# The opening of a two-layer decoder trunk: each gate unit for both token tiles in turn, and one product in native float32

## The chip, the core and the metric

The program runs on one core of one Trainium2 chip. The metric is the device time of one execution in microseconds (us); the time before is 909.27 us, the median of three runs (908.61 to 909.62). Times inside an execution are counted from the start of its profiled span.

## What is computed

Two layers, each of three sub-layers on 256 tokens of 1024 numbers: a SwiGLU feed-forward block, a mixer with parallel heads, and a second feed-forward block. Every sub-layer has a norm ahead of it and behind it.

```python
def _swiglu(h, wg, wu, wd):
    return (jax.nn.silu(h @ wg) * (h @ wu)) @ wd

for l in range(DEPTH):                       # DEPTH 2, D_MODEL 1024, D_FF 2816, SEQ 256
    f = _swiglu(_rmsnorm(h, ff1_norm_pre[l]), ff1_w_gate[l], ff1_w_up[l], ff1_w_down[l])
    h = h + 0.5 * _rmsnorm(f, ff1_norm_post[l])
    m = _hybrid_mixer(_rmsnorm(h, mix_norm_pre[l]), ...)
    h = h + _rmsnorm(m, mix_norm_post[l])
    f = _swiglu(_rmsnorm(h, ff2_norm_pre[l]), ff2_w_gate[l], ff2_w_up[l], ff2_w_down[l])
    h = h + 0.5 * _rmsnorm(f, ff2_norm_post[l])
```

All is float32. The change touches only the first columns of `h @ wg` and `h @ wu` in the first feed-forward block of the first layer, the first thing that the kernel does.

## The kernel before

**Split products.** A float32 operand is held as two tiles in a shorter format, an upper part `hi` (a copy into float32r by ScalarE, ACT, L117) and a lower part `lo` (the difference, by VectorE, DVE, L118). A product is then three: x-upper by `hi`, x-lower by `hi`, x-upper by `lo`. The x side is split too, into the two halves of `xT` (L258 on ACT, L259 on DVE). Every weight goes through ACT and DVE once on its way to the matrix engine (PE).

**Units and buffers.** Weights come in units of 1 MB (128 x 2048) by DMAs issued on the SyncE queue (SP, L85) into five `raw` buffers; a load waits until its buffer's last unit has been read. `Weights.split_next` splits the next unit into one of five `hi`/`lo` pairs; the units of the opening are split in four pieces of 512 columns, later ones in two of 1024.

**The opening.** The 256 tokens are two tiles t=0 and t=1 of 128. Per tile the normed x is turned by PE (L309, four 128x128 transposes into one PSUM bank, for each of two halves of the 1024 features). The first four units are the first 512 gate columns (units 0 and 1, for the two halves of the features) and the first 512 up columns (units 2 and 3). `ffn_first(t)` makes for one tile the gate product with units 0 and 1, then the up product with units 2 and 3 (`mm_half`, L398, 24 matmuls of 128x512 for each product), takes the SiLU of the first on ACT (L500) and multiplies on DVE (L490, the gate; its result is `hf`). All of tile 0 is made first, then all of tile 1. PE turns tile 1's x during tile 0's up product. Ahead of the first product PE runs six and later five matmuls on zeros (L233), which only keep it busy.

**Behind the opening.** The next four products (`ffn_quad`, L607) are a Strassen-like scheme: its weight units are sums (DVE, L113 and L136, in place in a `raw` buffer, then split like the others), its x operands are sums of quarters of x, split into tiles `n` (L258, L259); these come from copies `left` of tile 0's turned x and from tile 1's PSUM banks. Between the first and the second of these products PE turns the second tile's `hf` (`turn_tile`, L548), so its queue waits there for the second gate. The first tile's `hf` is turned by a DMA (`send`, L524) instead.

**What sets the order.** Each engine runs its own queue in the order in which the build's scheduler put the instructions; `tc.issue_after` and `tc.keep_in_program_order` constrain it. What stands in a queue can be read from the built program.

Of the kernel before, what the change touches and what calls it, by code (L numbers as in the profile page):

```python
# [10 lines left out]
F32 = mybir.dt.float32  # L11
# [3 lines left out]
AF = mybir.ActivationFunctionType  # L15
ALU = mybir.AluOpType
AX = mybir.AxisListType

P = 128
# [150 lines left out]
def hybrid_trunk_kernel(ctx: ExitStack, tc: tile.TileContext, a, out: bass.AP):  # L170
# [128 lines left out]
            nc.vector.scalar_tensor_tensor(xn[i], h[:, t, s], r, gain[i] if gain else gains[:, 0, s], op0=ALU.mult, op1=ALU.mult)  # L299
        return xn  # L300

    def pre_turn(t, xn, left=None, between=None):


        turned = []
        for i in range(2):
            ps = bank()
            for k in range(4):
                pre_turn.last = nc.tensor.transpose(ps[:, k * P : (k + 1) * P], xn[i][:, k * P : (k + 1) * P], ident)  # L309
            at = (slice(None), slice(4 * i, 4 * i + 4), slice(t * P, (t + 1) * P))  # L310
            split_into(xT, at, ps.rearrange("p (k n) -> p k n", k=4))
            pre_turn.lower = split_into.lower
            turned.append(ps)
            if between and not i:
                between()

        def keep():
            for i in range(2):
                left[i] = buf()
                nc.scalar.activation(left[i], turned[i], AF.Copy)  # L320

        if left is None:
            return
        if t == 0:
            return keep if between else keep()

        def part(name, x):
            left[name] = (buf(F32R, tag="n"), buf(F32R, tag="n"))
            split_into(left[name], (slice(None), slice(None)), x)
            left[name] = [y.rearrange("p (k n) -> p k n", k=4) for y in left[name]]  # L330

        s1, s3 = buf(), buf()
        x11, x12 = left.pop(0), left.pop(1)

        def rest():
            part("S3", s3)
            nc.vector.tensor_tensor(x12, x12, x11, op=ALU.add)
            part("S4", x12)

        def middle():  # L340
            part("S1", s1)
            nc.vector.tensor_tensor(x11, s1, x11, op=ALU.subtract)
            part("S2", x11)

        nc.scalar.activation(s1, turned[1], AF.Copy)
        nc.vector.tensor_tensor(s1, turned[0], s1, op=ALU.subtract)
        nc.vector.tensor_tensor(s3, x11, turned[0], op=ALU.subtract)
        left["middle"], left["rest"] = middle, rest
        for i, (name, k, t_) in enumerate((("X11", 0, 0), ("X12", 4, 0), ("X22", 4, 1))):
            left[name] = [x[:, k : k + 4, t_ * P : (t_ + 1) * P] for x in xT]  # L350
# [33 lines left out]
            for k in range(KD):  # L384
                nc.tensor.matmul(ps, x[:, k, s], w[:, k, :], start=i == 0 and k == 0, stop=i == 2 and k == KD - 1)  # L385

    def mm_half(ps, us, t, pin=False, ahead=None):


        for h, u in enumerate(us):  # L390
            hi, lo = (w[:, :UNIT].rearrange("p (k n) -> p k n", k=4) for w in W.get(u))
            x = [y[:, 4 * h : 4 * h + 4, t * P : (t + 1) * P] for y in xT]
            parts = [(k, i) for i in ((0, 2, 1) if pin else (0, 1, 2)) for k in range(4)]
            for n, (k, i) in enumerate(parts):
                if ahead and h == 1 and n == 8:
                    ahead()
                y, w = ((x[0], hi), (x[0], lo), (x[1], hi))[i]
                m = nc.tensor.matmul(ps, y[:, k, :], w[:, k, :], start=h == 0 and n == 0,  # L398
                                     stop=h == 1 and n == len(parts) - 1)
                if pin:  # L400
                    tc.keep_in_program_order(m)
            if t == NT - 1:
                W.done(u)
        return m
# [85 lines left out]
        nc.vector.tensor_tensor(hf, pu, s, op=ALU.mult)  # L490
        return hf

    def ffn_first(t, p, pin=False, ahead=None, between=None, by_dma=False):

        ps = [bank(), bank()]
        for i in range(2):
            mm_half(ps[i], [p["f", i, k] for k in range(2)], t, pin, ahead if i else None)
            if not i:
                s = buf()
                nc.scalar.activation(s, ps[0], AF.Silu)  # L500
        hf = gate(*ps, s)
        with tc.issue_after(pre_turn.lower.ins):
            if between:
                W.split_next()
                between()

            W.pump(SPLIT_BUFS - t)
        return send(hf) if by_dma else hf

# [187 lines left out]
    def ffn(l, n, p, gain, turned, left, next_left, before_next, last, later=None):  # L697
# [5 lines left out]
        def two(i):  # L703
            return i == QUADS[-1] or i == QUADS[1] or i == QUADS[0] and not start

        hf = [ffn_first(0, p, later is not None, turned, by_dma=by_dma)]
        middle = left.pop("middle")
        if later is None:
            middle()
        hf.append(ffn_first(1, p, between=middle if later else None))  # L710

        def down(i, t, behind=None):
            if acc[t] is None:
# [519 lines left out]
    xn0 = pre_scale(0, gain)  # L1233
    xn1 = pre_scale(1, gain)
    left = {}
    def first_unit():
        with tc.issue_after(split_into.last.ins):
            W.split_next()

    with tc.issue_after(norm_factor.last.ins):  # L1240
        keep = pre_turn(0, xn0, left=left, between=first_unit)
    busy(5, pre_turn.last.ins)
    with tc.issue_after(split_into.last.ins):
        W.split_next()
    with tc.issue_after(W.act.ins):
        W.split_next()
    with tc.issue_after(W.act.ins):
        W.split_next()
    with tc.issue_after(W.act.ins):
        keep()  # L1250

    turned = lambda: pre_turn(1, xn1, left=left)

    def later():
        with tc.issue_after(W.dma.ins):
# [130 lines left out]
```

## Time and profile before

| | before |
|---|---|
| median of three runs | 909.27 us |
| the profiled execution, its own time | 909.77 us |
| its span, first to last instruction | 908.1 us |
| PE busy | 898.9 us, 99% |
| DVE busy | 794.4 us, 87% |
| ACT busy | 673.1 us, 74% |
| first weight load of the first product (L398) | 11.00 us |
| first weight load of the first quad product (L607) | 35.09 us |
| end of the last matmul | 901.71 us |

PE is matmul work, PEld the loading of the stationary operand, which overlaps it. A row of the timeline gives the start, the time to the end of the last, the engine, the line, the operation, out<-in without buffer numbers, how many were merged, and in brackets how long the engine had stood idle before and what released it. Matmuls follow each other faster than one takes from start to end, so the pitch is read from the starts. PEclk is the clock that PE was granted, 1.00 being full.

### The profile page before, as it was taken

Reading aid. Unit: us, or ns where it says so; the run is one execution under the profiler, and the core shown is the slowest. Engines: PE = TensorE matmul, PEld = TensorE weight load, DVE = VectorE, ACT = ScalarE, POOL = GpSimd, SP = SyncE. Lnnn points to the kernel's source line nnn. Section 1 sums busy time; section 2 is a strip of 40 time slices with the busy share of each in tenths; the row PEclk is TensorE's granted clock in tenths of the full one; section 3 lists DMA queues with packets and bytes.
Section 4 is the critical chain, followed back from the end, with each engine's and each line's share of the span. In section 5 each row is a group of like instructions: output and inputs, shape, how many; then the busy total and the mean of one; then the engine's idle time right before and its main releaser. Section 6 shows DMA issues by size and latency. Waiting matters only on the chain.

```text
span 908.1 us, 12014 instructions
## 1 busy us (share of the span) xinstructions
PE 898.9 (99%) x4428; PEld 754.0 (83%) x4428; DVE 794.4 (87%) x1044; ACT 673.1 (74%) x1037; POOL 29.9 (3%) x49
## 2 busy tenths in 40 slices
PE   8999999999999999999999999999999999999997
PEld 5888888889988888888888888888998888888885
DVE  6999988789878998988799989887989699989882
ACT  7776777778858777777778678777797668778762
POOL 0000000000001000000000000000000110000000
PEclk9999999999999999999999999999999999999999
DMA  9679988765345589779655978794824246978741
GB/s 353 179 280 257 356 216 295 240 228 189 91 184 212 125 309 234 278 180 298 229 192 150 337 212 294 216 317 163 301 102 166 90 174 179 336 213 290 210 116 47
DMA packets 69326, 200.70 MB, mean 221 GB/s; under 512 B 44306, under 2 KB 44818, under 8 KB 47252
## 3 DMA queue, kind: packets, MB, share of 16 engines
q1 hardware_dynamic: 67396, 187.23, 60.9%
q0 software_dynamic: 1728, 12.58, 7.3%
q8 instruction: 35, 0.57, 0.2%
q14 instruction: 23, 0.19, 0.1%
q10 hardware_dynamic: 144, 0.13, 0.0%
HBM read 188.65 MB, written 1.05 MB: 209 GB/s over the span
## 4 chain that ended last, share of the span: by engine, by line
PE 93%; DVE 4%; issue 2%; DMA 1%; ACT 0%; POOLq 0%; SPq 0%; POOL 0%; DVEq 0%
PE acc L420 29%; PE wk L607 24%; PE wk L398 13%; PE wk L564 10%; PE wk L358 6%; PE wk L367 3%; DVE lo L118 2%; PE wk L369 2%; PE wk L385 1%; PE wk L309 1%; DMA raw<-in_ff_f 1%; PE wk L1146 1%; PE acc L889 0%; DVE raw L113 0%; PE acc L959 0%
## 5 line engine op out<-in xcount | busy, mean ns | idle before, releaser
L118 DVE TENSOR_TENSOR lo<-raw,hi 128x1024 fp32r<-128x1024 f32 (+2 forms) x452 | 465.4, 1076 | 30.0 <-ACT hi L117 29.4
L117 ACT ACTIVATE hi<-raw 128x1024 fp32r<-128x1024 f32 (+2 forms) x452 | 399.9, 936 | 68.4 <-DVE raw L113 34.2
L420 PE MATMUL acc<-hi,t 128*128 128x512 f32 x832 | 214.8, 391 | 0.0
L420 PEld LDWEIGHTS acc<-hi,t 128*128 128x128 f32 x832 | 155.2, 188 | 32.0 <-ACT t L258 0.3
L420 PE MATMUL acc<-lo,t 128*128 128x512 f32 x416 | 113.4, 390 | 0.0
L607 PE MATMUL wk<-hi,n 128*128 128x512 f32 x384 | 100.5, 390 | 0.0
L398 PE MATMUL wk<-hi,xT 128*128 128x512 f32 x384 | 98.9, 394 | 0.2
L420 PEld LDWEIGHTS acc<-lo,t 128*128 128x128 f32 x416 | 78.0, 188 | 16.3
L398 PEld LDWEIGHTS wk<-hi,xT 128*128 128x128 f32 x384 | 71.0, 188 | 16.4 <-ACT hi L117 1.6
L607 PEld LDWEIGHTS wk<-hi,n 128*128 128x128 f32 x384 | 71.8, 188 | 14.7
L607 PE MATMUL wk<-hi,xT 128*128 128x512 f32 x288 | 77.1, 390 | 0.1
L113 DVE TENSOR_TENSOR raw<-raw,raw 128x1024 f32<-128x1024 f32 x56 | 67.2, 1216 | 0.4
L524 ACT ACTIVATE t<-t 128x1024 uint16<-128x1024 uint16 x39 | 41.2, 1055 | 31.8 <-DVE t L685 20.6
L564 PE MATMUL wk<-hi,xT 128*128 128x512 f32 x256 | 64.5, 389 | 0.0
L607 PEld LDWEIGHTS wk<-hi,xT 128*128 128x128 f32 x288 | 54.0, 188 | 11.6 <-DVE t L647 0.4
L564 PEld LDWEIGHTS wk<-hi,xT 128*128 128x128 f32 x256 | 48.1, 188 | 10.0
L537 ACT ACTIVATE t<-t 128x1024 uint16<-128x1024 uint16 x35 | 47.9, 1367 | 8.5 <-DMA t<-t 8.5
L607 PE MATMUL wk<-lo,n 128*128 128x512 f32 x192 | 52.1, 390 | 0.0
L398 PE MATMUL wk<-lo,xT 128*128 128x512 f32 x192 | 52.1, 392 | 0.0
L398 PEld LDWEIGHTS wk<-lo,xT 128*128 128x128 f32 x192 | 36.0, 188 | 8.4 <-DVE lo L118 0.8
L358 PE MATMUL wk<-xT,hi 128*128 128x256 f32 x320 | 42.5, 284 | 0.0
L607 PEld LDWEIGHTS wk<-lo,n 128*128 128x128 f32 x192 | 36.0, 188 | 7.7 <-DVE lo L118 0.2
(190 smaller groups left out, 994.9 us busy)
## 6 DMA issues: line engine op xcount, KB each, us to landing
raw<-in_ff_q SPq DMA_DIRECT2D x48, 1024.0 KB, 6.8
raw<-in_ff_d SPq DMA_DIRECT2D x44, 1024.0 KB, 4.9
raw<-in_ff_f SPq DMA_DIRECT2D x16, 1024.0 KB, 7.6
raw<-in_ff_p SPq DMA_DIRECT2D x16, 1024.0 KB, 4.8
raw<-in_ff_q POOLq DMA_DIRECT2D x12, 1024.0 KB, 10.6
raw<-in_w_in SPq DMA_DIRECT2D x10, 1024.0 KB, 5.0
raw<-in_w_kvz SPq DMA_DIRECT2D x8, 1024.0 KB, 6.3
raw<-in_w_out SPq DMA_DIRECT2D x8, 1024.0 KB, 5.6
```

The lines of the kernel that those rows point to most:

```text
L113: nc.vector.tensor_tensor(raw[:, s], self.raw[x][:, s], self.raw[y][:, s], op=op)
L117: self.act = nc.scalar.activation(hi[:, s], raw[:, s], AF.Copy)
L118: nc.vector.tensor_tensor(lo[:, s], raw[:, s], hi[:, s].bitcast(F32), op=ALU.subtract)
L358: nc.tensor.matmul(ps, w[:, k, s], y[:, k, :], start=i == 0 and k == 0, stop=i == 2 and k == KD - 1)
L367: nc.tensor.matmul(ps, hi[:, k, s], both[:, :, k, :], start=k == 0, stop=k == KD - 1)
L369: mm_side.end = nc.tensor.matmul(ps[:, S:], lo[:, k, s], xT[0][:, k, :], start=False, stop=k == KD - 1, skip_group_check=True)
L398: m = nc.tensor.matmul(ps, y[:, k, :], w[:, k, :], start=h == 0 and n == 0, stop=h == 1 and n == len(parts) - 1)
L420: m = nc.tensor.matmul(acc[b], x[:, j, s], w[:, j, b * 512 : (b + 1) * 512], start=first and j == 0 and i == 0, stop=last and j == 1 and i ...
L524: part = send.last = nc.scalar.activation(halves.rearrange("p (a n) -> p a n", a=2), x[:, :].bitcast(U16).rearrange("p (n a) -> p a n", a= ...
L537: nc.scalar.activation(x[:, :].bitcast(U16).rearrange("p (n a) -> p a n", a=2), turned.rearrange("p (a n) -> p a n", a=2), AF.Copy)
L564: m = nc.tensor.matmul(ps[t], y[:, c, :], w[:, c, :], start=k == 0 and n == 0, stop=k == 1 and n == len(parts) - 1)
L607: nc.tensor.matmul(ps, x[:, k, :], w[:, k, :], start=first and n == 0, stop=n == len(parts) - 1, skip_group_check=not first)
```

## The change

`ffn_first` no longer makes the opening of the first block; a new function, `ffn_opening`, does (it is for this one block; the others keep `ffn_first`). What is different in it:

- Gate units go over both tiles in turn, up units tile by tile: unit 0 with tile 0, unit 0 with tile 1, unit 1 with tile 0, unit 1 with tile 1, then the up product of tile 0 and the up product of tile 1, each with units 2 and 3. Two gate sums are open at once, `pg[0]` in a `wk` bank and `pg[1]` in an `acc` bank.
- Unit 0 with tile 0 (`whole`) is four native float32 matmuls on the raw unit and on `left[0]`, the unsplit copy of tile 0's turned x, in place of twelve on split parts.
- Tile 1's x is turned in two parts: the first half between the second and the third of these four, the second half between unit 1's products with tile 0 and tile 1.
- In the three groups of four of each gate and up product the x-lower group comes before the `lo` group, for both tiles.
- The copies `left`, the splits of x and of the units stand in another order on ACT and DVE.

```diff
-        hf = [ffn_first(0, p, later is not None, turned, by_dma=by_dma)]
-        middle = left.pop("middle")
-        if later is None:
-            middle()
-        hf.append(ffn_first(1, p, between=middle if later else None))
+        if later:
+            hf = ffn_opening(p, turned, left)
+        else:
+            hf = [ffn_first(0, p, turned, by_dma=by_dma)]
+            left.pop("middle")()
+            hf.append(ffn_first(1, p))
...
+        def whole(ks, first):
+            w = W.raw[0][:, :UNIT].rearrange("p (k n) -> p k n", k=4)
+            for k in ks:
+                m = nc.tensor.matmul(pg[0], left[0][:, k * P : (k + 1) * P], w[:, k, :], start=first and k == 0, stop=False)
+                tc.keep_in_program_order(m)
+            return m
...
+        busy(5, turn.last.ins)
+        with behind(keep.last):
+            upper_part(0, 0)
+        pg = [bank(), bank("acc")]
+        whole((0, 1), True)
+        turn(1, 0)
+        whole((2, 3), False)
+        with behind(upper_part.last):
+            W.split_next()
+        with behind(W.act):
+            upper_part(1, 0)
+            keep(1)
+            lower_part(1, 0)
+            upper_part(0, 1)
+            lower_part(0, 1)
+        half(pg[1], 0, 0, 1, True, False)
+        with behind(upper_part.last):
+            W.split_next()
+        half(pg[0], 0, 1, 0, False, True)
+        turn(1, 1)
+        with behind(W.act):
+            upper_part(1, 1)
+            lower_part(1, 1)
+            lower_part(0, 0)
+        half(pg[1], 0, 1, 1, False, True)
+        s = [buf(), buf()]
+        nc.scalar.activation(s[0], pg[0], AF.Silu)
...
+        quarters(left, turned[1])
+        W.pump()
+        middle = left.pop("middle")
+        pu = [bank(), bank()]
+        for t in range(NT):
+            for h in range(2):
+                half(pu[t], 1, h, t, not h, bool(h))
+            hf = gate(None, pu[t], s[t])
+            if not t:
+                sent = send(hf)
+                W.split_next()
+                middle()
+        W.pump(SPLIT_BUFS - 1)
+        return [sent, hf]
```

`turn(t, i)` is four transposes (L496), `upper_part` an ACT copy into `xT`'s upper half (L506), `lower_part` the DVE difference (L510), `keep` the ACT copy into `left` (L514), `half` twelve matmuls (L522), `quarters` what stood at the end of `pre_turn`; the SiLUs are L569 and L574, the gate is L486, the quad product L700 and the transposes of the second `hf` L641.

The first place is PE's queue around the turning of tile 1's second half. Before, from the up product of tile 0 on (`wk30` is that product's bank, `wk39` the gate product of tile 1, `n23` and `n24` tile 1's normed x):

```order
L398 MATMUL wk30_219<-hi3_204,xT_108 128x512 x8
L309 MATMUL wk32_266<-ident_82,n23_151 128x128 x4
L309 MATMUL wk33_273<-ident_82,n24_152 128x128 x4
L398 MATMUL wk30_219<-lo3_205,xT_108 128x512 x4
L398 MATMUL wk39_315<-hi0_162,xT_108 128x512 x4
L398 MATMUL wk39_315<-lo0_163,xT_108 128x512 x4
L398 MATMUL wk39_315<-hi0_162,xT_108 128x512 x4
```

Now, from the first product on (`wk28` is `pg[0]`, `acc29` is `pg[1]`):

```order
L532 MATMUL wk28_173<-raw0_110,t27_165 128x512 x2
L496 MATMUL wk30_177<-ident_82,n23_151 128x128 x4
L532 MATMUL wk28_173<-raw0_110,t27_165 128x512 x2
L522 MATMUL acc29_174<-hi0_184,xT_108 128x512 x8
L522 MATMUL acc29_174<-lo0_185,xT_108 128x512 x4
L522 MATMUL wk28_173<-hi1_212,xT_108 128x512 x8
L522 MATMUL wk28_173<-lo1_213,xT_108 128x512 x4
L496 MATMUL wk32_234<-ident_82,n24_152 128x128 x4
L522 MATMUL acc29_174<-hi1_212,xT_108 128x512 x8
L522 MATMUL acc29_174<-lo1_213,xT_108 128x512 x4
```

The second half of the turn had four matmuls between it and its first user; now its user is the next instruction.

The second place is DVE's queue around the gate of the second tile (`t42` before, `t46` now). Before, from the split of unit 5 on:

```order
L118 TENSOR_TENSOR lo5_370<-raw4_291,hi5_369 128x1024 x2
L342 TENSOR_TENSOR t27_214<-t34_280,t27_214 128x512
L136 TENSOR_TENSOR raw4_291<-raw4_291,raw6_295 128x1024
L490 TENSOR_TENSOR t42_367<-wk40_316,t41_341 128x512
L259 TENSOR_TENSOR n46_384<-t27_214,n45_383 128x512
L136 TENSOR_TENSOR raw4_291<-raw4_291,raw6_295 128x1024
L118 TENSOR_TENSOR lo6_388<-raw4_291,hi6_387 128x1024
L118 TENSOR_TENSOR lo7_396<-raw7_297,hi7_395 128x1024
```

Now, from the last split of tile 1's x on (`wk32` is the bank of its second half):

```order
L510 TENSOR_TENSOR xT_108<-wk32_234,xT_108 128x4x128
L118 TENSOR_TENSOR lo2_258<-raw2_114,hi2_257 128x512 x4
L118 TENSOR_TENSOR lo3_268<-raw3_116,hi3_267 128x512 x4
L344 TENSOR_TENSOR t35_278<-wk30_177,t35_278 128x512
L345 TENSOR_TENSOR t36_279<-t27_165,wk30_177 128x512
L118 TENSOR_TENSOR lo4_294<-raw4_283,hi4_293 128x512 x4
L113 TENSOR_TENSOR raw4_283<-raw4_283,raw5_285 128x1024 x2
L486 TENSOR_TENSOR t39_346<-wk37_320,t33_254 128x512
L118 TENSOR_TENSOR lo5_304<-raw4_283,hi5_303 128x1024 x2
L136 TENSOR_TENSOR raw4_283<-raw4_283,raw6_287 128x1024 x2
L259 TENSOR_TENSOR n43_359<-t35_278,n42_358 128x512
```

and the rows that follow these:

```order
L118 TENSOR_TENSOR lo6_313<-raw4_283,hi6_312 128x1024
L118 TENSOR_TENSOR lo7_353<-raw7_289,hi7_352 128x1024
L118 TENSOR_TENSOR lo6_313<-raw4_283,hi6_312 128x1024
L118 TENSOR_TENSOR lo7_353<-raw7_289,hi7_352 128x1024
L340 TENSOR_TENSOR t27_165<-t35_278,t27_165 128x512
L486 TENSOR_TENSOR t46_391<-wk38_321,t34_255 128x512
```

The second gate stood between the two pieces of the second weight sum (L136); it now stands behind both pieces and behind the splits of units 6 and 7.

The third place is PE's queue at the turning of the second tile's `hf`. Before and now, in this order:

```order
L607 MATMUL wk47_403<-hi4_301,xT_108 128x512 x4
L548 MATMUL wk49_418<-ident_82,t42_367 128x128 x4
L607 MATMUL wk55_433<-hi5_369,n43_378 128x512 x4
```

```order
L700 MATMUL wk47_395<-hi4_293,xT_108 128x512 x4
L641 MATMUL wk49_410<-ident_82,t46_391 128x128 x4
L700 MATMUL wk55_425<-hi5_303,n42_358 128x512 x4
```

Nothing moved here: the transposes still stand between the first and the second quad product, and read the second gate.

More of the change, by code (lines that the diff above doesn't have):

```diff
@@ L300, in pre_scale, with pre_turn @@
         return xn
-    def pre_turn(t, xn, left=None, between=None):
+    def pre_turn(t, xn, left=None):
         turned = []
@@ L313, in pre_turn @@
             turned.append(ps)
-            if between and not i:
-                between()
-        def keep():
+        if left is None:
+            return
+        if t == 0:
             for i in range(2):
@@ L320, in keep, with quarters @@
                 nc.scalar.activation(left[i], turned[i], AF.Copy)
-        if left is None:
             return
-        if t == 0:
-            return keep if between else keep()
+        quarters(left, turned)
+    def quarters(left, turned):
         def part(name, x):
@@ L385, in mm_tok, with mm_half @@
                 nc.tensor.matmul(ps, x[:, k, s], w[:, k, :], start=i == 0 and k == 0, stop=i == 2 and k == KD - 1)
-    def mm_half(ps, us, t, pin=False, ahead=None):
+    def mm_half(ps, us, t, ahead=None):
         for h, u in enumerate(us):
@@ L392, in mm_half @@
             x = [y[:, 4 * h : 4 * h + 4, t * P : (t + 1) * P] for y in xT]
-            parts = [(k, i) for i in ((0, 2, 1) if pin else (0, 1, 2)) for k in range(4)]
+            parts = [(k, i) for i in range(3) for k in range(4)]
             for n, (k, i) in enumerate(parts):
@@ L399, in mm_half @@
                                      stop=h == 1 and n == len(parts) - 1)
-                if pin:
-                    tc.keep_in_program_order(m)
             if t == NT - 1:
@@ L495, in ffn_first @@
+    def ffn_first(t, p, ahead=None, by_dma=False):
         ps = [bank(), bank()]
         for i in range(2):
-            mm_half(ps[i], [p["f", i, k] for k in range(2)], t, pin, ahead if i else None)
+            mm_half(ps[i], [p["f", i, k] for k in range(2)], t, ahead if i else None)
             if not i:
@@ L502, in ffn_first @@
         with tc.issue_after(pre_turn.lower.ins):
-            if between:
-                W.split_next()
-                between()
             W.pump(SPLIT_BUFS - t)
@@ L1235, in hybrid_trunk_kernel @@
     left = {}
[L1236 to L1252, printed above, removed]
+    turned = [xn0, xn1]
     def later():
```

44 lines of the change are left out of this document (43 added, 1 removed).

## The prediction

> **What bounds the kernel now.** I read the page first, then the busy time by stretch, then the waits of the weight loader, and last the timeline of the first 45 us.
>
> ```profile
> PE 898.9 (99%) x4428; PEld 754.0 (83%) x4428; DVE 794.4 (87%) x1044; ACT 673.1 (74%) x1037; POOL 29.9 (3%) x49
> ```
>
> PE is the bound. By stretch (start:end, length, then PE, PEld, DVE, ACT and POOL busy with counts, PEclk, DMA share, GB/s):
>
> ```profile
> 11.00:35.10 24.10, 24.05 (x104) 18.62 (x105) 22.67 (x35) 17.86 (x31) 1.03 (x1) 1.00 0.85 321
> 35.10:120.00 84.90, 84.81 (x378) 69.72 (x377) 82.04 (x86) 65.73 (x78) 0.88 (x1) 1.00 0.84 271
> ```
>
> DVE has hardly a free microsecond in either: 22.67 of 24.10 and 82.04 of 84.90. So whatever PE loses there is lost to the end, and whatever stands late in DVE's queue arrives late. The weight loader's waits between 10 and 70 us show what little PE does lose:
>
> ```profile
> PEld wk L398 <- ACT hi L117: 1.6, 4, 0.6
> PEld wk L398 <- DVE lo L118: 0.8, 2, 0.4
> PEld wk L607 <- DVE t L647: 0.4, 1, 0.4
> PEld wk L607 <- DVE lo L118: 0.2, 1, 0.2
> ```
>
> The first two are the opening, where PE starts behind the splits. The last two come at about 61 us.
>
> **The opening on PE.** Rows of PE, PEld, ACT and, in the first, of the chain that ended last:
>
> ```profile
> 2.68 7.61 DMA raw<-in_ff_f
> ...
> 9.46 0.58 ACT L258 ACTIVATE xT<-wk 128x512 fp32r<-128x512 f32 x1
> ...
> 9.51 0.85 PEld L233 LDWEIGHTS <-zeros 128*128 128x128 bf16 x5
> ...
> 11.00 0.19 PEld L398 LDWEIGHTS wk<-hi,xT 128*128 128x128 f32 x1 [0.64 <-ACT hi L117]
> ...
> 22.38 1.03 PEld L309 LDWEIGHTS wk<-ident,n 128*128 128x128 f32 x8
> ...
> 23.25 1.09 ACT L258 ACTIVATE xT<-wk 128x512 fp32r<-128x512 f32 x2 [1.30 <-PE wk L309]
> ...
> 35.09 0.87 PEld L607 LDWEIGHTS wk<-hi,xT 128*128 128x128 f32 x4
> ...
> 37.81 0.59 PEld L548 LDWEIGHTS wk<-ident,t 128*128 128x128 f32 x4
> ```
>
> From 35.09 to 37.81 PE does twelve matmuls: 0.227 us each, 2.72 for twelve. Before, the opening is 96 of them (21.8) and eight transposes (1.0 from the row at 22.38): 22.8 of the 24.09 us from 11.00 to 35.09. The other 1.3 are stalls.
>
> The change takes away twelve matmuls (2.72) and puts in four of native float32. Their price:
>
> ```profile
> 6.57 0.34 PEld L1231 LDWEIGHTS acc<-n,n 128*128 128x128 f32 x1 [0.52 <-issue]
> 7.42 0.15 PEld L233 LDWEIGHTS <-zeros 128*128 128x128 bf16 x1 [0.52 <-issue]
> ```
>
> ```profile
> 254.81 1.02 PE L1185 MATMUL acc<-t,vec 128*128 128x256 f32 x4
> ```
>
> ```profile
> L1185 PE MATMUL acc<-t,vec 128*128 128x256 f32 x8 | 2.0, 378 | 0.0
> ```
>
> The pooled product L1185 is two native products per layer on 256 columns and shows four records, two for each; their pitch is (1.02 - 0.378) / 3 = 0.214. So 512 columns cost 2 x 0.43 = 0.86. The only native product with 512 columns (L1231) shows 7.42 - 6.57 = 0.85 per record, 1.71 per product, but at the opening's low speed; by 9.51 the fills of 512 columns follow each other within 0.85 / 4 = 0.21. The new product comes after those fills, so I take 0.86, 3.43 for four: 0.7 more than it replaces. The other end would add 3.4.
>
> In return PE need not wait for splits. The raw unit lands at 2.68 + 7.61 = 10.29; the unsplit copy is made where the first x split stands now, 9.46 to 10.04; the loader is through with the fills at 10.36 and their columns keep PE a little longer. I start the first product at 10.6, against 11.00.
>
> Then one new wait. The second half of tile 1's turn is followed at once by its user. In the row at 23.25 ACT starts 0.87 behind the start of the transposes at 22.38; its copy takes 0.58. The user can go on 1.48 after the turn's start; the four transposes fill 0.5 of that, so PE stands for 1.0. Behind PE's waiting instruction is queued everything else of the opening, and DVE waits for the same copy.
>
> The sum on PE: 10.6 + 3.43 + 0.5 (first half of the turn) + 24 x 0.227 (5.45) = 19.98, start of the second half; 1.48 later, 21.46, unit 1 with tile 1 goes on; 2.72 for it and 10.88 for the four up halves give 35.06 for the first quad product. Before: 35.09. The float32 product and the bare turn eat what the earlier start and the missing stalls give: the opening itself comes out even, within 0.6 either way.
>
> **The second gate on DVE.** This is where I see the change's price. PE reaches the transposes of the second `hf` at 35.06 + 2.72 = 37.78. Before, the gate that they read was ready in time:
>
> ```profile
> 15.14 7.30 DVE L118 TENSOR_TENSOR lo<-raw,hi 128x512 fp32r<-128x512 f32 x12
> ...
> 35.03 1.22 DVE L136 TENSOR_TENSOR raw<-raw,raw 128x1024 f32<-128x1024 f32 x1
> 36.16 0.68 DVE L490 TENSOR_TENSOR t<-wk,t 128x512 f32<-128x512 f32 x1
> 36.76 0.68 DVE L259 TENSOR_TENSOR n<-t,n 128x512 fp32r<-128x512 f32 x1
> ...
> 38.50 4.62 DVE L118 TENSOR_TENSOR lo<-raw,hi 128x1024 fp32r<-128x1024 f32 x4
> ```
>
> It ended at 36.84, and the transposes were loaded at 37.81. The pitch of a DVE row of 512 columns is (7.30 - 0.68) / 11 = 0.60, of 1024 columns (4.62 - 1.22) / 3 = 1.13.
>
> Now DVE's queue has, from tile 1's last lower part on, which can start when ACT's copy ends, at 21.46: fifteen rows of 512 columns (that one, three units' four pieces, L344, L345), 9.0; two sums, the first gate, two splits of unit 5, two more sums, `n43`, four splits of units 6 and 7, L340: ten rows of 1024 (11.3) and three of 512 (1.8). Only then the gate, 0.68. It ends at 21.46 + 9.0 + 11.3 + 1.8 + 0.7 = 44.3. Nothing lets DVE begin that chain earlier, since its first row waits for the turn; from about 18 us on DVE stands idle for it, where before it was splitting units 2 and 3.
>
> So PE's transposes, and in order behind them everything else of PE's queue, wait from 37.8 to 44.3: 6.5 us behind the 37.81 of before. A cross-check from the other side: ahead of the gate there are now one sum and four splits more, 5.7, and DVE's idle time is about 2 longer than before, less 1 for the gate's old slack. And both ends hang on the same turn, so an error in the opening's 19.98 moves the two together and hardly changes the wait.
>
> At about 61 us the two stalls of before (0.6 in the loader, of which I count 0.5) should vanish, since DVE, ACT and the loads have then run ahead of PE: 6.5 - 0.5 = 6.0.
>
> **The clock.** A wait that long has a price of its own. The clock around the end of the kernel, same columns as above, and the last matmuls:
>
> ```profile
> 901.80:905.60 3.80, 0.00 (x0) 0.00 (x0) 2.29 (x5) 0.92 (x3) 0.55 (x1) 1.00 0.15 57
> 905.70:908.10 2.40, 0.00 (x0) 0.00 (x0) 0.00 (x0) 0.00 (x0) 0.00 (x0) 0.50 0.35 114
> ```
>
> ```profile
> 901.09 0.62 PE L420 MATMUL acc<-hi,t 128*128 128x512 f32 x2
> ```
>
> PE's last matmul ends at 901.71, and 3.9 to 4.0 us later the granted clock is 0.50. The wait here leaves PE idle for over 6. So I expect half speed when PE goes on. How long:
>
> ```profile
> 2.32 0.13 PEld L233 LDWEIGHTS <-zeros 128*128 128x128 bf16 x2 [2.32 <-DVE zeros L222]
> ```
>
> PE's first work is at 2.32, and the step from 6.57 to 7.42 is still at 0.85: at least 5.1 us of work at half speed. 5.1 at half speed loses 2.5. Bounds: 0 if the clock stays, and (9.51 - 2.32) / 2 = 3.6.
>
> The Trainium skill, "TensorE: Matmul & The Clock Gate", Part 1, says that the monitor looks at free-running windows of about 3.4 us, halves the clock after an idle one and restores it after a busy one. By that rule an idle stretch of 6.2 us holds a whole window in about 8 of 10 phases, and half speed then lasts 3.4 to 6.8 us, an estimate of 1.7 to 3.4 us lost. The 3.9 us at the end of this trace agree with it.
>
> **What costs nothing.** Unit 7's load now waits for unit 2's later split, and the DMA that adds into unit 5's buffer (POOL) for the later sums:
>
> ```profile
> raw<-in_ff_d SPq DMA_DIRECT2D x44, 1024.0 KB, 4.9
> ...
> raw<-in_ff_q POOLq DMA_DIRECT2D x12, 1024.0 KB, 10.6
> ```
>
> Unit 2 is split by 21.46 + 0.6 + 2.4 = 24.5, so unit 7 lands at about 29.4 and is read at 38; the sums are done at 32.7, the added unit lands at 43.3 and is read behind the wait. Both are covered by 5 us or more; without that cover each would cost what it is late. The first `hf` is sent by DMA from 33.5 on, and is wanted only behind the wait.
>
> **The sum.** 909.77 (the profiled execution) + 6.5 - 0.5 + 2.5 = 918.3; that execution was 0.5 over the median of its runs, so 917.8 against 909.27.
>
> **The rivals.** *The clock stays.* The same wait without the half speed: 909.27 + 6.0 = 915.3. For it: only one idle stretch with its clock is in this trace, and the wait begins 0.3 late, while the last matmul drains. Against it: 3.9 us sufficed there.
>
> *Faster: the gate is in time.* If the rows ahead of it took DVE no more than 37.78 - 21.46 = 16.3 us, PE would not stand there, the opening would come out even, and the 0.5 at 61 us might still be saved: 908.8, or 907.8 if the turn hides behind unit 0's work too. That needs rows at 16.3 / 22.8 = 0.72 of their measured pitch. The pitches are those of the same rows on the same sizes, so I give it little.
>
> *No change that can be seen.* DVE is late by a microsecond, the 61 us stall gives it back: 909.3. It needs nearly the same speed.
>
> *Slower still.* The chain behind the gate (L335, `n45`, ACT's `n44`) or a native product at half speed (+3.4) adds to the wait: 921.
>
> **How the numbers follow.** The wait with half speed 0.70, the wait at full clock 0.18, slower still 0.05, faster 0.04, no change 0.03. The likeliest gives 917.8. The range holds the first two: down to 915.3 less 0.6 for the opening, 914.7; up to 909.27 + 6.5 + 3.6 + 0.4 = 919.8. A measurement of this kernel tells about 0.2%, 1.8 us, from no change: faster 0.04, same 0.03, slower 0.93.
>
> **What would show it.** In the new timeline: the float32 product as eight PE records 0.43 apart from about 10.7; 1.0 of idle on the loader ahead of L522, released by ACT L506; the first L700 at 35.1; then the largest wait of the trace, PE L641 on DVE L486, 6 to 7 us long, with DVE unbroken ahead of it; PEclk below 1.00 in the stretch from about 42 to 49, and matmuls 0.43 apart there. I am wrong if L641 waits under 2 us, or if the matmuls behind the wait keep 0.227.

## The result, and the profile after

The changed kernel takes 916.87 us, the median of five runs (916.15 to 917.63), against 909.27 before (five runs, 908.61 to 909.62). The ratio is 1.0082 with a 95% interval of 1.0071 to 1.0093: slower by 7.6 us. The profiled execution took 917.63 us with a span of 915.9. Where readings of it are set against the profiled execution of before, the difference to explain is 7.86 (917.63 less 909.77).

The page's line of busy times, in the order of before's:

```profile
PE 899.6 (98%) x4424; PEld 755.0 (82%) x4424; DVE 794.6 (87%) x1044; ACT 673.4 (74%) x1037; POOL 29.9 (3%) x49
```

PE is busy 0.7 us longer than before and the span is 7.8 longer, so by this count 7.1 us are idle PE. (Slow matmuls count as busy, and so does part of the short stalls of before, since the ends of matmuls are modelled; the stretches below tell more than the total.) The weight loader's waits from 8 to 120 us name the place (line, waited for: us in total, times, longest):

```profile
PEld wk L641 <- DVE t L486: 6.7, 1, 6.7
PEld acc L522 <- ACT xT L506: 1.0, 1, 1.0
```

Before, the longest wait from 10 to 70 us was 0.6 long. Now one of 6.7 stands at the second gate, and one of 1.0 at the bare turn. The two stalls of before at 61 us are gone from the list. PE's timeline, with start, busy time and the idle time before it:

```profile
10.25 1.95 PE L532 MATMUL wk<-raw,t 128*128 128x512 f32 x4
...
12.48 1.88 PE L532 MATMUL wk<-raw,t 128*128 128x512 f32 x4
...
21.03 2.11 PE L522 MATMUL acc<-hi,xT 128*128 128x512 f32 x8 [0.74 <-ACT xT L506]
...
34.77 1.07 PE L700 MATMUL wk<-hi,xT 128*128 128x512 f32 x4
...
43.93 1.11 PE L641 MATMUL wk<-ident,t 128*128 128x128 f32 x4 [6.28 <-DVE t L486]
44.70 2.05 PE L700 MATMUL wk<-hi,n 128*128 128x512 f32 x4
46.55 1.91 PE L700 MATMUL wk<-lo,n 128*128 128x512 f32 x4
...
51.64 1.07 PE L700 MATMUL wk<-hi,n 128*128 128x512 f32 x4
52.55 0.61 PE L416 MATMUL acc<-hi,t 128*128 128x512 f32 x2
```

Read downwards: the float32 product is eight records, two groups of four, with the turn of tile 1's first half between them. A group is two products of 512 columns and takes 1.9, where four split matmuls at L700 take 1.07, both with their drain. The opening is done at 34.77. Then PE waits 6.28 us for the gate, and afterwards four matmuls take 2.05 and 1.91 instead of 1.07, until normal speed is back in the last row of the product. DVE around its idle time and around the gate:

```profile
21.01 0.69 DVE L510 TENSOR_TENSOR xT<-wk,xT 128x512 fp32r<-128x512 f32 x1 [3.12 <-ACT xT L506]
...
35.18 2.35 DVE L136 TENSOR_TENSOR raw<-raw,raw 128x1024 f32<-128x1024 f32 x2
...
38.05 4.62 DVE L118 TENSOR_TENSOR lo<-raw,hi 128x1024 fp32r<-128x1024 f32 x4
42.60 0.68 DVE L340 TENSOR_TENSOR t<-t,t 128x512 f32<-128x512 f32 x1
43.20 0.68 DVE L486 TENSOR_TENSOR t<-wk,t 128x512 f32<-128x512 f32 x1
```

DVE stands idle for 3.12 us for the turn, then has no gap until the gate at 43.20. The two sums (2.35) and four pieces of units 6 and 7 (4.62) stand directly ahead of it. The granted clock is in the stretches behind (start:end, length, then busy times of PE, PEld, DVE, ACT and POOL with counts, PEclk, DMA share, GB/s):

```profile
42.00:44.00 2.00, 0.07 (x1) 0.07 (x2) 2.00 (x4) 0.63 (x1) 0.00 (x0) 0.68 0.39 65
45.00:48.00 3.00, 3.00 (x9) 2.32 (x8) 3.00 (x5) 2.89 (x4) 0.00 (x0) 0.50 0.60 254
48.00:50.00 2.00, 2.00 (x7) 1.54 (x6) 2.00 (x3) 1.08 (x3) 0.00 (x0) 0.61 0.00 0
50.00:53.00 3.00, 3.00 (x14) 2.44 (x13) 1.94 (x3) 3.00 (x5) 0.00 (x0) 1.00 0.00 0
```

A mean of 0.68 over the first two microseconds is 1.3 us at half speed, so the clock fell at about 42.7, a good microsecond before PE went on, and the mean of 0.61 from 48 to 50 puts its return at about 49.6. PE's rows say the same: four matmuls take 1.85 us from 44.70 to 46.55, 0.46 each, where full speed takes 0.227. (The counts of a stretch include matmuls that only reach into it.)

### The profile page after: what moved, and what is told of

The parts are those of the page before. It is cut to its first block, busy times and chain, and to the rows that moved or that the text cites. A ratio compares the mean times of both kernels' runs of the same rounds, so it can differ in the third digit from the quotient of the medians.

```text
span 915.9 us, 12006 instructions
## 1 busy us (share of the span) xinstructions
PE 899.6 (98%) x4424; PEld 755.0 (82%) x4424; DVE 794.6 (87%) x1044; ACT 673.4 (74%) x1037; POOL 29.9 (3%) x49
## 4 chain that ended last, share of the span: by engine, by line
PE 95%; DVE 3%; issue 1%; ACT 0%; POOLq 0%; POOL 0%; DVEq 0%
PE acc L416 30%; PE wk L700 25%; PE wk L396 12%; PE wk L657 10%; PE wk L356 6%; PE wk L365 3%; PE wk L367 2%; DVE lo L118 1%; PE wk L383 1%; PE wk L309 1%; PE wk L1240 1%; PE acc L983 0%; PE acc L233 0%; PE wk L532 0%; PE acc L1053 0%
## 5 line engine op out<-in xcount | busy, mean ns | idle before, releaser
L118 DVE TENSOR_TENSOR lo<-raw,hi 128x1024 fp32r<-128x1024 f32 (+2 forms) x452 | 465.9, 1076 | 35.9 <-ACT hi L117 35.1
L117 ACT ACTIVATE hi<-raw 128x1024 fp32r<-128x1024 f32 (+2 forms) x452 | 399.7, 937 | 75.1 <-DVE raw L113 31.7
L416 PE MATMUL acc<-hi,t 128*128 128x512 f32 x832 | 214.7, 390 | 0.0
L416 PEld LDWEIGHTS acc<-hi,t 128*128 128x128 f32 x832 | 155.3, 188 | 31.8
L416 PE MATMUL acc<-lo,t 128*128 128x512 f32 x416 | 113.4, 390 | 0.0
L700 PE MATMUL wk<-hi,n 128*128 128x512 f32 x384 | 102.0, 395 | 0.0
L416 PEld LDWEIGHTS acc<-lo,t 128*128 128x128 f32 x416 | 77.9, 188 | 16.3
L700 PEld LDWEIGHTS wk<-hi,n 128*128 128x128 f32 x384 | 72.9, 191 | 15.2
L396 PE MATMUL wk<-hi,xT 128*128 128x512 f32 x320 | 81.9, 392 | 0.0
L700 PE MATMUL wk<-hi,xT 128*128 128x512 f32 x288 | 77.0, 389 | 0.0
L396 PEld LDWEIGHTS wk<-hi,xT 128*128 128x128 f32 x320 | 59.0, 188 | 12.5 <-ACT xT L258 0.7
L657 PE MATMUL wk<-hi,xT 128*128 128x512 f32 x256 | 64.8, 389 | 0.0
L700 PEld LDWEIGHTS wk<-hi,xT 128*128 128x128 f32 x288 | 54.1, 188 | 11.2
L657 PEld LDWEIGHTS wk<-hi,xT 128*128 128x128 f32 x256 | 48.0, 188 | 9.9
L700 PE MATMUL wk<-lo,n 128*128 128x512 f32 x192 | 52.7, 394 | 0.0
L700 PEld LDWEIGHTS wk<-lo,n 128*128 128x128 f32 x192 | 36.6, 191 | 7.8
L396 PE MATMUL wk<-lo,xT 128*128 128x512 f32 x160 | 42.9, 390 | 0.0
L356 PEld LDWEIGHTS wk<-xT,hi 128*128 128x128 f32 x320 | 40.5, 191 | 0.7
```

The source lines that it names most:

```text
L117: self.act = nc.scalar.activation(hi[:, s], raw[:, s], AF.Copy)
L118: nc.vector.tensor_tensor(lo[:, s], raw[:, s], hi[:, s].bitcast(F32), op=ALU.subtract)
L356: nc.tensor.matmul(ps, w[:, k, s], y[:, k, :], start=i == 0 and k == 0, stop=i == 2 and k == KD - 1)
L416: m = nc.tensor.matmul(acc[b], x[:, j, s], w[:, j, b * 512 : (b + 1) * 512], start=first and j == 0 and i == 0, stop=last and j == 1 and i ...
L657: m = nc.tensor.matmul(ps[t], y[:, c, :], w[:, c, :], start=k == 0 and n == 0, stop=k == 1 and n == len(parts) - 1)
L700: nc.tensor.matmul(ps, x[:, k, :], w[:, k, :], start=first and n == 0, stop=n == len(parts) - 1, skip_group_check=not first)
```

## The experiments

The theory (A): the opening comes out even, PE loses its time in the wait for the late second gate, and half speed behind the wait is a term of its own. The main rival (B): the opening itself loses the time, by the float32 product and the two turns, and a gate in time would only move the wait. A second pair concerns the clock: is its price real, and how long an idle time halves it? Medians in us, each beside the kernel before as it ran on the same chip in the same batch. The changed kernel itself stands in none of these batches, so a difference from its 916.87 holds the shift between batches too; where that matters, the difference is also given with each kernel set against its own kernel before (7.6 us for the changed kernel).

| run | median | before | ratio, 95% interval |
|---|---|---|---|
| e1_gate_ahead | 910.65 | 908.90 | 1.0020 (1.0011 to 1.0029) |
| e2_fills | 914.39 | 908.90 | 1.0059 (1.0046 to 1.0072) |
| e3_split_first | 912.66 | 908.90 | 1.0043 (1.0031 to 1.0056) |
| e4_turn_early | 910.18 | 908.90 | 1.0014 (1.0005 to 1.0022) |
| e5_split_ahead | 909.44 | 908.98 | 1.0006 (0.9997 to 1.0015) |
| e6_split_alone | 914.67 | 908.98 | 1.0061 (1.0049 to 1.0074) |
| e7_best_no_f32 | 911.41 | 908.98 | 1.0025 (1.0014 to 1.0036) |
| e8_sum_early | 908.07 | 908.83 | 0.9988 (0.9979 to 0.9997) |
| e9_fills_half | 912.84 | 908.83 | 1.0037 (1.0025 to 1.0050) |
| e10_fills_pinned | 914.85 | 908.68 | 1.0067 (1.0054 to 1.0080) |
| e11_turn_later | 913.62 | 908.68 | 1.0056 (1.0042 to 1.0070) |
| e12_fills_18 | 916.12 | 908.68 | 1.0081 (1.0067 to 1.0095) |

### The gate ahead of the sums (e1_gate_ahead)

```diff
-        nc.vector.tensor_tensor(hf, pu, s, op=ALU.mult)
+        gate.last = nc.vector.tensor_tensor(hf, pu, s, op=ALU.mult)
...
         quarters(left, turned[1])
-        W.pump()
+        W.pump(splits=1)
...
-        W.pump(SPLIT_BUFS - 1)
+        pump_behind(gate.last, SPLIT_BUFS - 1)
```

> The changed kernel with the second gate taken out from behind the sums: two of the later sums' pieces and the splits of units 6 and 7 now stand behind it on VectorE, nothing on TensorE moves. Theory A (the loss is TensorE's wait for the late gate, 6.7 us in the changed kernel's profile, and the half clock that follows it, 2.3 us): the L641 wait falls below 1 us, the granted clock stays at 1.00 from 38 to 50 us, and the time falls from 916.9 to between 908.5 and 911; what is left above the kernel before would be waits of the second quad product (L700) of up to 1.5 us for the parts of units 6 and 7, which are split later now. Rival B (the loss lies in the opening itself, in the float32 product and the two turns): the wait moves to another place and the time stays at 916 to 917.

It took 910.65, 6.2 less than the changed kernel, or 5.85 with each against its own kernel before. The loader's waits, largest first, from 8 to 120 us:

```profile
PEld wk L700 <- DVE lo L118: 1.3, 2, 1.0
PEld acc L522 <- ACT xT L506: 1.0, 1, 1.0
...
PEld wk L700 <- ACT hi L117: 0.8, 1, 0.8
PEld acc L416 <- DVE t L259: 0.4, 1, 0.4
PEld wk L700 <- DVE t L740: 0.4, 1, 0.4
```

No wait of L641 for the gate is left. Behind it 2.9 us have come: 0.8 and 1.0 in the quad product on unit 6 for that unit's parts (the third; the expectation counts it as the second, from the transposes on), 0.4 in the first down product (L416) for the lower part of an `hf`, and 0.7 at about 63 us, where the stalls of before were. The changed kernel's wait and half speed, 6.7 and 1.4 to 2.7 (measured below), less these 2.9, make 5.2 to 6.5; measured 5.85 to 6.2. The opening of this kernel is the changed kernel's, float32 product and bare turn in it: theory A holds and B falls. What came behind was put at up to 1.5 and is nearly double.

### Unit 2's split ahead of the turn (e6_split_alone)

```diff
         with behind(W.act):
+            W.split_next()
+        with behind(W.act):
             upper_part(1, 1)
             lower_part(1, 1)
             lower_part(0, 0)
...
         with behind(upper_part.last):
             W.split_next()
-        with behind(W.act):
-            W.split_next()
         nc.scalar.activation(s[1], pg[1], AF.Silu)
```

> The changed kernel with one step moved: unit 2's split stands on ScalarE and VectorE ahead of tile 1's second half instead of behind it, in the 3.1 us for which VectorE stands idle there in the changed kernel. The gate keeps its place behind the sums and the splits of units 6 and 7. Four pieces at 0.60 us, 2.4 us, then leave the chain from the turn to the gate. Theory A (the gate is late by the rows that VectorE does between the turn and it, whatever they are): the wait of L641 falls by 2.4, from 6.7 to 4.3 us, and the time by 2.4 to about 914.5, and by another 2.3 to about 912.2 in runs in which 4.3 us of idle TensorE are too short to halve the clock. Rival B (what delays the gate is a transfer or ScalarE, not VectorE's rows): the wait and the time stay, 916 to 917.

It took 914.67, 2.2 less (1.9 with each against its own kernel before). DVE at the turn and at the gate, and the wait:

```profile
20.47 0.69 DVE L510 TENSOR_TENSOR xT<-wk,xT 128x512 fp32r<-128x512 f32 x1 [1.02 <-ACT xT L506]
...
40.24 0.68 DVE L486 TENSOR_TENSOR t<-wk,t 128x512 f32<-128x512 f32 x1
```

```profile
PEld wk L641 <- DVE t L486: 4.3, 1, 4.3
```

The idle time fell from 3.12 to 1.02. From the row behind it to the gate DVE now takes 19.8 us (20.47 to 40.24) instead of 22.2 (21.01 to 43.20), and the wait fell from 6.7 to 4.3, both by the 2.4 us of the four pieces. So the gate is late by DVE's rows. The clock halved here too, after a shorter idle time; PE's row of L641, and the granted clock while PE stood:

```profile
40.98 1.12 PE L641 MATMUL wk<-ident,t 128*128 128x128 f32 x4 [3.87 <-DVE t L486]
```

```profile
38.00:40.00 2.00, 0.00 (x0) 0.00 (x0) 2.00 (x3) 0.00 (x0) 0.00 (x0) 0.96 0.68 67
```

PE had ended its last matmul at 37.11 (40.98 less 3.87). A mean of 0.96 from 38 to 40 puts the fall at about 39.8, only 2.7 us later.

### The price of the half clock (e2_fills, e9_fills_half, e10_fills_pinned)

```diff
-        turn()
         pc = bank()
+        if not by_opening:
+            turn()
+        else:
+            for _ in range(26):
+                m = nc.tensor.matmul(pc, zeros[:, :P], zeros, start=True, stop=True)
+                tc.keep_in_program_order(m)
+            turn()
```

> The changed kernel with 26 matmuls on zeros (bfloat16, 512 columns, 0.21 us each, 5.6 us in all) put on TensorE between the first quad product and the second gate's transposes, written into a bank that the next product overwrites. The gate's way on VectorE is unchanged, so TensorE stands no less behind it, only busy. Theory A (the half clock behind the idle wait is a term of its own): the granted clock stays at 1.00 from 38 to 53 us, the matmuls behind the gate keep 0.22 us, the remaining wait of L641 is about 1 us, and the time falls by the 2.3 us, from 916.9 to about 914.5. Rival B (the slower matmuls hide behind other waits, only the gate counts): 916.9, unchanged.

914.39, as theory A had it, but for a reason that was not wholly the right one. PE's rows show that five matmuls of the second quad product now stood ahead of the transposes:

```profile
37.78 5.79 PE L717 MATMUL wk<-zeros 128*128 128x512 bf16 x26
43.21 1.27 PE L700 MATMUL wk<-hi,n 128*128 128x512 f32 x4
44.32 0.40 PE L700 MATMUL wk<-lo,n 128*128 128x512 f32 x1
44.56 0.60 PE L641 MATMUL wk<-ident,t 128*128 128x128 f32 x4
```

They did 1.1 us of useful work inside the wait (five at 0.227). With 13 matmuls on zeros (`range(13)`) all twelve went ahead:

> As e2_fills, with 13 instead of 26 matmuls on zeros ahead of the second gate's transposes: TensorE is busy for 2.8 us of the wait and idle for the last 3.6 or so. In e6_split_alone 3.9 us of idle TensorE were followed by half speed. Theory A (the clock is judged in stretches of fixed length, so an idle time a little longer than one of them halves it only where it happens to cover one): the clock drops in some runs or in none, and the time is 914.4 in most, 1.7 to 2.4 more in the others. Theory B (any idle time of 3 us or more halves it): all runs lie at 916 to 917.

```profile
37.37 2.75 PE L717 MATMUL wk<-zeros 128*128 128x512 bf16 x12
39.77 1.28 PE L700 MATMUL wk<-hi,n 128*128 128x512 f32 x4
40.88 1.07 PE L700 MATMUL wk<-lo,n 128*128 128x512 f32 x4
41.80 1.07 PE L700 MATMUL wk<-hi,n 128*128 128x512 f32 x4
43.54 0.66 PE L641 MATMUL wk<-ident,t 128*128 128x128 f32 x4 [0.68 <-DVE t L486]
```

912.84, below both forecasts, since the idle time that it was to leave did not come about: 2.75 of fills and 2.7 of useful product filled the wait. It says nothing on the clock by itself. So the first was repeated with the order on PE held fixed (the same edit, and `keep_in_program_order` for the transposes and the product as well):

> The 26 matmuls on zeros of e2_fills again, with the order of TensorE held fixed behind them: the transposes of the second gate, then the second quad product. In e2_fills five matmuls of that product, in e9_fills_half all twelve, had moved ahead of the transposes and done useful work in the wait, so neither run gave the price of the half clock alone. Theory A (half speed costs what the trace shows, 2.3 us): 914.5 against 916.9, the wait being filled to 1 us. Rival B (half speed costs little, since later waits absorb it; the gain of the two earlier runs was the moved matmuls): 916 to 917.

```profile
37.70 5.56 PE L723 MATMUL wk<-zeros 128*128 128x512 bf16 x25
43.88 0.65 PE L641 MATMUL wk<-ident,t 128*128 128x128 f32 x4 [0.61 <-DVE t L486]
...
49.85 1.07 PE L416 MATMUL acc<-hi,t 128*128 128x512 f32 x4
```

914.85: 2.0 below the changed kernel by the medians, 1.4 with each against its own kernel before. In the traces, from the start of the transposes to the first L416, it takes 5.97 us (49.85 less 43.88) at full speed against 8.62 (52.55 less 43.93): 2.65. The work there is the same, and the transposes start within 0.05 us of each other. The changed kernel's profiled execution is the slowest of its five, 0.76 over their median, so its trace gives the upper end; the 95% intervals of the two ratios just overlap (1.0071 to 1.0093 and 1.0054 to 1.0080), so the medians alone do not settle the size. The half clock costs 1.4 to 2.7, and no later wait absorbs it: the two profiled executions differ by 2.8 in all (917.63 and 914.85).

### How long an idle time halves the clock (e11_turn_later, e12_fills_18)

In e11_turn_later the second gate's transposes stand behind the second quad product (the last argument of `product` and `turn_tile.pin` hold the order on PE fixed):

```diff
-        turn()
+        if not by_opening:
+            turn()
         pc = bank()
-        product(pc, left["S1"], p["T1", i], True)
+        product(pc, left["S1"], p["T1", i], True, by_opening)
+        if by_opening:
+            turn_tile.pin = True
+            turn()
+            turn_tile.pin = False
```

> The changed kernel with nothing filled in, but the second gate's transposes put behind the second quad product, which needs only the parts of unit 5: its twelve matmuls (2.72 us) then stand inside the wait for the gate. Theory A: the wait of L641 falls from 6.7 to 4.0, a wait of up to 1.4 us comes back at about 64 us, and the time falls by 1.5 to 2.7: to 914.2 to 915.4 if the 3.9 us of idle TensorE that remain still halve the clock, to 911.9 to 913.1 if not. Rival B (the wait is not for the gate's turn alone, the products wait as well): no change from 916.9.

```profile
43.49 1.11 PE L641 MATMUL wk<-ident,t 128*128 128x128 f32 x4 [3.56 <-DVE t L486]
```

913.62: 3.25 less than the changed kernel, 0.6 better than the case of half speed had been put at and 0.5 worse than the case of full speed. With each against its own kernel before it is 2.7 less, which is the edge of the case of half speed, so that the 0.6 may be no more than the shift between batches. The loader's wait is 4.0, no wait came back at 64 us, and half speed followed for a shorter time: the granted clock is 0.77 from 43 to 44 us, 0.50 from 44 to 46, 0.52 from 46 to 47 and 1.00 behind that, which is half speed from about 43.5 to about 47.

e12_fills_18 is e10_fills_pinned with `range(18)`.

> As e10_fills_pinned with 18 instead of 26 matmuls on zeros: TensorE is idle for the last 2.8 us of the wait. Theory A (2.8 us are too short to halve the clock, where 3.9 us did in e6_split_alone): full clock and 914.5, level with e10_fills_pinned. Theory B (already 2.8 us halve it, in some runs or all): up to 916.9.

916.03 to 916.36 in four runs, with a mean granted clock of 0.996 in each, against 0.998 or 0.999 in the runs of e10_fills_pinned: half speed came in all of them. PE's rows of the matmuls on zeros and of L641, and the granted clock around them:

```profile
37.42 3.83 PE L723 MATMUL wk<-zeros 128*128 128x512 bf16 x17
43.64 1.09 PE L641 MATMUL wk<-ident,t 128*128 128x128 f32 x4 [2.38 <-DVE t L486]
```

```profile
40.60:44.00 3.40, 1.02 (x6) 0.46 (x4) 3.40 (x5) 0.63 (x1) 0.00 (x0) 0.96 0.61 81
44.10:47.40 3.30, 3.30 (x11) 2.68 (x11) 3.30 (x5) 2.60 (x4) 0.00 (x0) 0.54 0.67 278
47.50:50.00 2.50, 2.50 (x13) 2.03 (x12) 1.50 (x4) 1.60 (x4) 0.00 (x0) 1.00 0.00 0
```

Theory A of that run falls: 2.4 us of idle PE halve the clock. A mean of 0.96 over the first 3.4 us is 0.27 us at half speed, so it falls at about 43.7, when PE has just resumed; a mean of 0.54 over the next 3.3 puts the return at about 47.1. The price is 1.3 (916.12 less 914.85, both of one batch). That is below the range after the long wait, as it should be when full speed is back after 3.4 us instead of 6.8; but it is so near its lower end that the medians do not show the difference by themselves.

### The float32 product by itself (e3_split_first, e7_best_no_f32)

```diff
-        whole((0, 1), True)
-        turn(1, 0)
-        whole((2, 3), False)
...
+            lower_part(0, 0)
+        half(pg[0], 0, 0, 0, True, False)
+        turn(1, 0)
```

> As the run with the gate ahead (e1_gate_ahead), but the float32 product is undone: unit 0 with tile 0 is made of twelve matmuls on split parts, the turn of tile 1's first half behind it. Against e1_gate_ahead it tells the price of the float32 product alone. Theory A (four float32 matmuls cost 3.43 for 2.72, and start earlier because no split is waited for; together even): the time lies 0 to 1.4 us above e1_gate_ahead. Rival B (the float32 product costs more than it gives): it lies 0.7 to 3.4 us below e1_gate_ahead.

> As e5_split_ahead, but with the float32 product undone, as in e3_split_first: twelve matmuls on split parts for unit 0 with tile 0. It repeats the price of that product where no late gate follows. By e3_split_first against e1_gate_ahead the float32 product gives 2.0 us: here the time should lie 1.4 to 2.0 us above e5_split_ahead. If the 2.0 came only from what followed it there, the two are level within 0.5.

912.66 is 2.0 above e1_gate_ahead, 911.41 is 2.0 above e5_split_ahead. The float32 product gives 2.0 us in both places, more than theory A had put it at in the first. The loader in e3_split_first shows why:

```profile
11.46 0.19 PEld L522 LDWEIGHTS wk<-hi,xT 128*128 128x128 f32 x1 [1.83 <-ACT hi L117]
...
16.73 0.76 PEld L522 LDWEIGHTS acc<-hi,xT 128*128 128x128 f32 x4 [1.13 <-ACT xT L506]
17.89 0.76 PEld L522 LDWEIGHTS acc<-hi,xT 128*128 128x128 f32 x4 [0.40 <-DVE xT L510]
```

Without it PE starts at 11.46 instead of 10.59 (e1_gate_ahead's first load of L532; the matmuls on zeros are loaded at 8.78 in both). It then stands about 1.0 more between the pieces of unit 0's split (the loader's list has 2.8 in four waits for ACT L117, the longest 1.8). And the first half of tile 1's turn is bare as well: 1.13 and 0.40 of waits that otherwise lie behind the second half of the float32 product. Less the 0.7 that this product takes longer, that makes 2.7; the first load of L700 is 2.5 later (37.44 against 34.90), and the two profiled executions differ by 2.6.

### The turn early, the split ahead, the sums early (e4, e5, e8)

```diff
             for n, (y, w) in enumerate(((x[0], hi), (x[1], hi), (x[0], lo))):
+                if ahead and n == 2:
+                    ahead()
                 for k in range(4):
...
-        half(pg[0], 0, 1, 0, False, True)
-        turn(1, 1)
+        half(pg[0], 0, 1, 0, False, True, lambda: turn(1, 1))
```

> As e1_gate_ahead, but the transposes of tile 1's second half stand ahead of the last four matmuls of unit 1 with tile 0 instead of behind them, so that ScalarE's copy runs beside 0.9 us of TensorE's work. Theory A (the 1.0 us that TensorE stands behind that turn goes straight to the end, since VectorE's chain to the gate begins with the same copy): the wait of L522 for ScalarE falls from 1.0 to about 0.1 and the time lies 0.6 to 1.0 below e1_gate_ahead. Rival B (the time goes to a later wait instead, on the parts of units 6 and 7): the second quad product waits longer by as much, and the time is e1_gate_ahead's within 0.3.

The wait of L522 (L524 in this kernel) for ACT fell from 1.0 to 0.2, but the time only by 0.47, from 910.65 to 910.18: the wait of L700 (now L701) for DVE L118 grew from 1.3 to 1.6, and the gate was 0.2 late. Less than either bound of theory A, more than B. Adding e6_split_alone's edit:

> As e4_turn_early (gate ahead, turn early), with unit 2's split moved ahead of tile 1's second half on ScalarE and VectorE as in e6_split_alone. All rows of VectorE behind the turn come 2.4 us earlier, the parts of units 6 and 7 among them, for which the second quad product of e4_turn_early still waits 0.8 and 1.3 us. Theory A (VectorE's rows after the turn are the bound of the whole stretch): those waits go, some wait further down by the first hf's parts (up to 1 us) may stay, and the time falls from 910.2 to between 908 and 909.3, level with the kernel before or just below it. Rival B (what is left above the kernel before comes from elsewhere): 910 stays.

909.44, level with the kernel before, 0.14 above the interval's end that was expected. Waits left:

```profile
PEld acc L416 <- ACT t L258: 1.4, 1, 1.4
...
PEld acc L416 <- DVE t L259: 0.7, 1, 0.7
```

Those are for the first `hf`, whose parts ACT makes behind unit 6's and 7's splits. The last edit moves the two sums of unit 6 ahead of the second gate:

```diff
-        if i in self.whole:
+        if i in self.whole and self.summed < i:
...
                 W.split_next()
+                W.sum_next()
                 middle()
```

> As e5_split_ahead, with the two sums that make unit 6 moved on VectorE from behind the second gate to ahead of it (behind unit 5's split), so that ScalarE can split unit 6 in its idle time of 2.6 us at 34 us; in e5_split_ahead the first hf's parts, which the down product L416 waits for, stand on ScalarE behind that split. Theory A (what is left of the stretch are those waits of 1.1 and 0.4 us): both go, the gate is still ready when TensorE comes to it, and the time falls by 1.5 from 909.4 to about 908, 0.9 below the kernel before or 0.1%. Rival B (the sums ahead delay the gate as in the changed kernel): L641's transposes wait 1 us or more and the time stays at 909.4 or above.

```profile
32.31 2.36 DVE L136 TENSOR_TENSOR raw<-raw,raw 128x1024 f32<-128x1024 f32 x2
...
35.78 0.69 DVE L486 TENSOR_TENSOR t<-wk,t 128x512 f32<-128x512 f32 x1
```

```profile
36.52 0.51 PEld L643 LDWEIGHTS wk<-ident,t 128*128 128x128 f32 x4
```

The gate ends at 36.47 and the transposes are loaded at 36.52: in time, with both sums ahead of it, because the chain starts earlier, and no wait of L416 is left in the loader's list. 908.07 against 908.83: the ratio's interval, 0.9979 to 0.9997, leaves out 1. It is the only version that beats the kernel before, by 0.1%.

## Why the prediction was right

917.8 was forecast, 916.87 came, and the case was the likeliest one. Point by point:

- **Float32 product.** 0.86 each, eight records 0.43 apart from about 10.7. In the trace the records start at 10.25, and the loads follow each other at 0.43. Right; the other end (3.4 more) is excluded. The start was 0.35 early, with the matmuls on zeros, which are loaded at 8.85 in this execution (before at 9.51); from the first product to the first quad product PE took 24.52 us (34.77 less 10.25), forecast 24.46.
- **The bare turn.** 1.0 forecast, 1.0 on the loader. Right.
- **The opening comes out even, within 0.6.** The first load of L700 stands at 34.54, before at 35.09: 0.55 early. Right, but at the bound, and in part by when this execution began: in the eight profiled executions that have this opening on PE (the changed kernel, e1, e2, e6 and e9 to e12) the first load of L532 stands between 9.63 and 10.59 and that of L700 between 34.01 and 34.90, while the way from one to the other is 24.3 to 24.6 in all. What "the float32 product and the bare turn eat" was not shown term by term against the kernel before. Inside the new order the product gives 2.0, more than its 0.7 of debit and 0.4 of earlier start suggest; what these two leave out is that it hides the turn's first half and the stalls for unit 0's pieces.
- **The gate.** Forecast: 44.3, which is 9.2 behind the first quad product. Measured: 43.88, 9.3 behind it. The wait was put at 6.5 over before's 37.81; the loader waited 6.7 and was 6.1 later than before (43.93), the opening's 0.55 being the difference. Right, and e1_gate_ahead and e6_split_alone show that DVE's rows make it. "Nothing lets DVE begin that chain earlier" was true of the changed kernel's order only: e6_split_alone does 2.4 us of it ahead of the turn with one step moved.
- **61 us.** 0.5 given back: right, both stalls are gone.
- **The clock.** 2.5 forecast; 1.4 to 2.0 by the medians of e10_fills_pinned, 2.65 by its trace. That half speed follows and costs time was right; that the size fits so well is partly luck. The 5.1 us at half speed were a lower bound, read from the pitch at the kernel's start (the column PEclk reads 1.00 there), and nothing in that row says how long half speed lasts behind a wait. It lasted 6.8 us in the changed kernel, 5.6 of them with PE at work, and as long in e6_split_alone, but 3.4 in e11_turn_later and e12_fills_18, at a price of 1.3 in the last. The step behind it had a flaw that did not show in the number: the prediction took 3.9 us of idle PE as what is known to halve the clock, and 2.4 suffice (e12_fills_18). The rival with full clock therefore deserved less than its 0.18. The Trainium skill, "TensorE: Matmul & The Clock Gate", Part 1, from which 1.7 to 3.4 was estimated, speaks of windows of about 3.4 us that are idle or busy. The 2.65 of the trace lies in that estimate, and the two lengths of half speed are one and two such windows. Its condition that a window be idle is too strict here: the idle time of e12_fills_18 is a microsecond shorter than such a window, and in the 3.4 us ahead of its drop (40.3 to 43.7) PE worked for 0.9 us, until 41.25.
- **What costs nothing.** No wait for a transfer stands in the loader's list from 8 to 120 us. Right.
- **The sum.** In the profiled executions, by PE's rows of before (below) and of the changed kernel (above): the transposes start 5.9 later, the way from them to the first down product (L420 before, L416 now) is 2.7 longer (8.62 against 5.91), and 0.45 is won back at 61 us, where the lead of before falls from 8.60 to 8.14. That makes 8.15 against 7.86; the 0.3 over is small spread further down, which no run here assigns. The forecast had 6.5, 2.5 and -0.5. What it had too much at the gate, 0.6, is the early opening.

```profile
38.04 0.60 PE L548 MATMUL wk<-ident,t 128*128 128x128 f32 x4
...
43.95 1.07 PE L420 MATMUL acc<-hi,t 128*128 128x512 f32 x4
```

- **The rivals.** "The gate is in time" needed DVE rows at 0.72 of their pitch; four rows of 1024 columns took 4.62 in both traces.

## What to carry to other kernels

When an opening is reordered for PE, write down what the engine that feeds it has to do between its last forced wait and the next result that PE needs: here 22.8 us of rows, which PE's work covered for 16.3. The product that looked like the risk was a gain, 2.0 us inside the new order. An idle time of PE of 2.4 us, the shortest that halved the clock here, or more must be priced with the half speed that follows, 1.3 to 2.7 us here. An experiment that fills a wait must hold the order behind it fixed, or it measures the work that moves in.

## What was not expected of the hardware

The clock fell behind idle times of 6.28, 3.87, 3.56 and 2.38 us and stayed behind 0.68 and 0.61. The longest that it stayed behind is 1.33, ahead of the first product of e3_split_first: the granted clock is 1.00 from 10 to 14 us there, and the matmuls from 14.31 on follow each other at 0.23. For 2.38 it fell when PE had already resumed, and half speed then lasted 3.4 us; behind 6.28 it lasted from about 42.7 to about 49.6. Between 1.33 and 2.38 us nothing was measured.
